# Forgetting heads' queries and keys stored once per pair of heads; latent projections one chunk earlier

## The chip, the cores and the metric

The kernel runs on one core of one Trainium2 chip, as one launch. The metric is the time of that launch on the device in microseconds (us). Engine names are those of the profile: PE is the matrix engine and PEld its weight load, DVE the vector engine, ACT the scalar engine, POOL the general-purpose engine, SP the engine that issues nearly all transfers here (in the trace its issues are called SPq).

## The reference, cut to what matters

Two layers, each a mixer and a mixture of experts, over 1024 tokens of width 1024 in float32. The mixer has 16 heads of width 64: eight forgetting heads, whose scores get a decay from a running sum of log forget gates, and eight latent heads, whose queries, keys and values come from two small latents.

```python
proj = xn @ w_in                      # 3*512 forgetting q, k, v; 8 forget logits; latents of 256 and 128; 32 rope
log_f_cum = jnp.cumsum(log_sigmoid(f_logit + b_f), axis=1)
fox = causal_block_attention(fq, fk, fv, log_f_cum)      # s = q.k * scale + cum[q] - cum[k], softmax, values
q  = rms_norm(c_q) @ w_uq             # 8 heads of 64, plus 32 with rotary
kv = rms_norm(c_kv) @ w_ukv           # 8 heads of 64 keys and 64 values
mla = causal_block_attention(concat(q_nope, rot(q_rope)), concat(k_nope, rot(k_rope)), v)
h = h + concat(rms_norm(fox), rms_norm(mla)) @ w_o
h = h + hierarchical_moe(rms_norm(h), ...)               # 32 experts, two per token
```

## The kernel before, in words

Every float32 matrix product is done as three products of a high and a low part: the helper `split` (L181) makes them, the high part on ACT, the low part as a difference on DVE, and `mm3` (L190) issues the three products (L194, L195, L196). The order on PE, ACT, DVE and POOL is the order in which the program is written; transfers are issued by SP, one after the other.

A mixer goes through these stages, and the change touches the middle ones:

1. Norm, transposes and the small columns of `w_in`, into `xT[0]` and `xT[1]` (high and low parts of the normed input, transposed).
2. Six chunks of 256 columns of `w_in`, in the order v, v, q, q, k, k (L746). Each q or k chunk has four steps of 24 products of 512 columns: two pairs of heads by two halves of the tokens. After a step, `take` (L777) splits its 128 rows (two heads) into a staging tile `st` and writes them to DRAM. While a chunk is computed, `prepare` loads and splits the weights of the next one.
3. Between the steps, work is taken from a queue `jobs`: first the forget gates, latents and value scaling, and from the first k chunk on, when `late_pools` (L664) has opened their space, the latent projections: four loads of `w_uq`, two of `w_ukv`, and 20 projections (`nope` L722, `rope_a` L704, `rope_b` L714), whose results go to DRAM through the same kind of staging tile, called MQ, MQR and MK there.
4. After the last step, the operands of head 0 are loaded (`load_ops`, L806), the latent heads' values are computed in eight blocks of three products (L827 to L832), each copied out by ACT and scanned for its maximum by DVE (`v_take`), and head 1's operands are loaded. Two heads' operands fit at a time (`ops`, two buffers).
5. Attention: per unit of work, scores `S` (L873), row maximum `nm` (DVE, L885), exponential (ACT, L894), transposes (L902), values (L916). Head h+2 is loaded when head h's scores are done.

For forgetting head h the scores are two passes. The first contracts over 128 rows: the queries' high part twice, against the keys' low and high parts. The second contracts over 68 rows: the queries' low part against the keys' high part, and four rows that carry the decay and rows of ones. `FQ` and `FK` in DRAM hold these rows per head as they will be loaded: for the queries 64 rows high, 64 rows high again, 64 rows low, 4 rows; for the keys 64 low, 64 high, 4 rows. So each head's queries are written as two transfers out of 64 rows of `st` (L786, L787), and loaded as one of 128 rows and one of 68 rows (L810 to L813):

```python
                move(o[:, 0], FQ[h, 0:2 * HD])          # 128 rows
                move(o[:, 2], FK[h, 0:2 * HD])
                move(o[0:HD + 4, 1], FQ[h, 2 * HD:])    # 68 rows
                move(o[0:HD + 4, 3], FK[h, HD:])
```

A latent head is loaded as four transfers of 64 or 32 rows with the high and low parts side by side (L816 to L819). The operands' space is that of `xT[1]`, so the load of head 0 waits for the last product that reads it. Eight semaphores are shared by all transfers of SP, so a transfer also waits for the one eight before it.

Of the kernel before, what the change touches and what calls it, by code (L numbers as in the profile page):

```python
# [10 lines left out]
F32R = mybir.dt.float32r  # L11
# [9 lines left out]
P = 128  # L21
T = 1024
# [4 lines left out]
H = 8  # L27
# [54 lines left out]
def kernel(ctx: ExitStack, tc: tile.TileContext, x, positions, attn_norm, w_in, b_f, q_norm, w_uq,  # L82
# [283 lines left out]
    def mixer(l, opened):  # L366
        h_in = [xv[i] for i in range(NT)] if l == 0 else h_d[2 * l - 1]
        h_out = h_d[2 * l]

        FQ = dram.tile([H, 3 * HD + 4, T], F32R, name=f"FQ{l}")  # L370
        FK = dram.tile([H, 2 * HD + 4, T], F32R, name=f"FK{l}")
        MQ = dram.tile([H * HD, 2, T], F32R, name=f"MQ{l}")
        MQR = dram.tile([H * RD, 2, T], F32R, name=f"MQR{l}")
        MK = dram.tile([H * HD, 2, T], F32R, name=f"MK{l}")
# [191 lines left out]
        def forget_d(c):  # L566
            ps = pp.tile([P, 512], F32, name="ps")
            for i in range(4):
                pe.transpose(ps[0:H, i * P:(i + 1) * P], fl["cum"][:, 4 * c + i], ident)
            cs = slice(c * 512, c * 512 + 512)  # L570
            for dst, sgn in ((FQ[:, 3 * HD + 2:, cs], None), (FK[:, 2 * HD:2 * HD + 2, cs], -1.0)):
                st = stg.tile([P, 2, 512], F32R, name="st")[0:H]
                split(st[:, 0], st[:, 1], ps[0:H], sgn)
                move(dst, st)
# [83 lines left out]
            return [v_max, *gap, lambda: v_scale(g, tp)] + [lambda i=i: v_split(g, i, src) for i in range(NT)]  # L658

        one = trix[0:H, None, P:].to_broadcast([H, 16, P])  # L660
        for dst in (FQ[:, 3 * HD:3 * HD + 2], FK[:, 2 * HD + 2:]):
            move(dst.rearrange("h r (c t) -> h (r c) t", t=P), one)

        def late_pools():  # L664
# [74 lines left out]
            for i, (j, c) in enumerate(jc):  # L739
                jobs.append(lambda j=j, c=c: rope_a(j, c))  # L740
                jobs.extend(qj[2 * i:2 * i + 2])
                jobs.append(lambda j=j, c=c: rope_b(j, c))
            jobs.extend(kj)

        late = {}
        chunks = [("v", 0), ("v", 1), ("q", 0), ("q", 1), ("k", 0), ("k", 1)]  # L746
# [3 lines left out]
        for ci, (nm, half) in enumerate(chunks):  # L750
            _, wh, wl = cur
            nxt = prepare(base[chunks[ci + 1][0]] + 256 * chunks[ci + 1][1]) if ci + 1 < len(chunks) else None
            if (nm, half) == ("k", 0):
                late_pools()
            if nm == "v":
                al = slice(0, 256)
                for i in range(NT):
                    ps = pp.tile([P, 512], F32, name="ps")
                    ts = slice(i * P, (i + 1) * P)
                    mm3(ps[:, :256], lambda k: xT[0][:, k, ts], lambda k: xT[1][:, k, ts],  # L760
                        lambda k: wh(k, al), lambda k: wl(k, al), range(KC))
                    if i % 2:
                        run(nxt[0], 2)
                    run(jobs, 2 if i % 2 else 1)
                    v_take(vraw[:, i, half * 256:half * 256 + 256], ps[:, :256], half * NT + i)
                if half == 1:
                    jobs.extendleft(reversed(v_jobs(0, vraw, pp, [lambda: None] * 2)))
            else:
                for s in range(4):
                    j, c = 2 * half + s // 2, s % 2  # L770
                    js, cs = slice((s // 2) * P, (s // 2 + 1) * P), slice(c * 512, c * 512 + 512)
                    ps = pp.tile([P, 512], F32, name="ps")
                    mm3(ps, lambda k: wh(k, js), lambda k: wl(k, js),
                        lambda k: xT[0][:, k, cs], lambda k: xT[1][:, k, cs], range(KC))
                    if nxt:
                        run(nxt[0], 2)
                    def take(nm=nm, j=j, cs=cs, ps=ps):  # L777
                        st = stg.tile([P, 2, 512], F32R, name="st")
                        if nm == "q":
                            split(st[:, 0], st[:, 1], ps, FOX_SCALE)  # L780
                        else:
                            split(st[:, 1], st[:, 0], ps)
                        for e in range(2):
                            h, rs = 2 * j + e, slice(e * HD, (e + 1) * HD)
                            if nm == "q":
                                move(FQ[h, HD:3 * HD].rearrange("(b r) t -> r b t", r=HD)[:, :, cs], st[rs])  # L786
                                move(FQ[h, 0:HD, cs], st[rs, 0])  # L787
                            else:
                                move(FK[h, 0:2 * HD].rearrange("(b r) t -> r b t", r=HD)[:, :, cs], st[rs])

                    if ci == len(chunks) - 1 and s == 3:
                        break
                    take()
                    run(jobs, 4 if nm == "k" else 3)
            cur = nxt
        ring_close()
        xp_close()
# [8 lines left out]
        def load_ops(hh):  # L806
            h = hh % H
            o = ops.tile([P, 4, T], F32R, name="op")
            if hh < H:
                move(o[:, 0], FQ[h, 0:2 * HD])  # L810
                move(o[:, 2], FK[h, 0:2 * HD])
                move(o[0:HD + 4, 1], FQ[h, 2 * HD:])
                move(o[0:HD + 4, 3], FK[h, HD:])  # L813
                return ((o[:, 0], o[:, 2], P), (o[:, 1], o[:, 3], HD + 4))
            hs, rs = slice(h * HD, (h + 1) * HD), slice(h * RD, (h + 1) * RD)
            move(o[0:HD, 0:2], MQ[hs])  # L816
# [2 lines left out]
            move(o[HD:MD, 2:4], MKR)  # L819
            return ((o[:, 0], o[:, 2], MD), (o[:, 0], o[:, 3], MD), (o[:, 1], o[:, 2], MD))  # L820

        opnd = {0: load_ops(0)}
        take()
        uk = late["uk"]
        mx8 = small.tile([P, 2 * NT], F32, name="mx8", bufs=2)
        dve.memset(mx8[:, 0:NT], 0.0)
        for i in range(NT):  # L827
# [2 lines left out]
            mm3(ps, lambda k: ckT[0][:, ts], lambda k: ckT[1][:, ts], lambda k: uk[0][:, 512:1024],  # L830
                lambda k: uk[1][:, 512:1024], [0])
            v_take(vraw2[:, i], ps, NT + i)  # L832
        run(jobs, len(jobs))
        opnd[1] = load_ops(1)
        late["close"]()
        raws_close()
# [859 lines left out]
```

## Time and profile before

| What | us |
|---|---|
| three runs | 1952.24, 1957.9, 1958.68 (median 1957.9) |
| the profiled execution | 1960.09 |
| its span, first to last instruction | 1958.3 |

The profile is of one execution; 1.8 us of it lie outside the span. Its engine line gives busy time, share of the span and number of instructions. In the timeline a row has a start, a duration, the engine, the line, the operation, the tiles (written <- read), partitions x elements, how many instructions were merged, and in brackets how long the engine sat idle before it and for whom. In a table by windows each engine has its busy time (with instructions in brackets), and the last columns are the granted clock of PE as a share of 2.4 GHz, the mean busy share of the 16 DMA engines and the GB/s that they moved.

### The profile page before, as it was taken

To read this page: it belongs to the slowest core of one execution; us is meant where nothing else is said; L and a number is where in the kernel's file an instruction comes from. 1 tells how busy PE (TensorE), PEld (TensorE's weight loads), DVE (VectorE), ACT (ScalarE), POOL (GpSimd) and SP (SyncE) were. 2 spreads that over 40 slices of the span, in tenths; PEclk is the share of its full clock that TensorE was granted. 3 is DMA by queue.
4 is the path that set the end of the run, shared out by engine and by line. 5 is a ranking of instruction groups with operands and counts; after the bars stand their busy time and mean duration, and the time that the engine had idled before them with its cause. 6 is when DMAs were issued, how large, how long until landed. Compare 5 with 4: busy or idle time off the path is not lost.

```text
span 1958.3 us, 33744 instructions
## 1 busy us (share of the span) xinstructions
PE 1745.1 (89%) x12509; PEld 1410.6 (72%) x12509; DVE 1366.3 (70%) x2172; ACT 1185.7 (61%) x2254; POOL 588.1 (30%) x857
## 2 busy tenths in 40 slices
PE   7999889999995999999499997999999869999960
PEld 6987678888884677666399876888878647776540
DVE  6463478888346999888565345888853579988865
ACT  4443378888212889888444335888851258987751
POOL 4001144233204343332231021623341333333215
PEclk9999989999997999999799998999999979999985
DMA  5247833453764999999841775344446569999975
GB/s 160 65 120 217 259 133 110 99 120 87 251 204 146 310 356 357 357 355 354 291 151 52 199 243 200 124 108 109 109 169 233 172 228 363 345 354 350 356 294 213
DMA packets 145380, 427.11 MB, mean 218 GB/s; under 512 B 22166, under 2 KB 37564, under 8 KB 142140
## 3 DMA queue, kind: packets, MB, share of 16 engines
q1 hardware_dynamic: 129788, 387.14, 60.1%
q0 software_dynamic: 14336, 33.58, 5.2%
q10 hardware_dynamic: 1088, 4.19, 0.6%
q8 instruction: 100, 1.64, 0.3%
q14 instruction: 68, 0.56, 0.1%
HBM read 347.24 MB, written 94.37 MB: 226 GB/s over the span
## 4 chain that ended last, share of the span: by engine, by line
PE 28%; DMA 14%; DVE 4%; ACT 3%; issue 2%; POOL 1%; SPq 0%; POOLq 0%; ACTq 0%; DVEq 0%
DMA gu<-in_w_gate_dram 5%; PE ps L194 5%; PE ps L195 5%; PE ps L196 5%; DMA gu<-in_w_up_dram 4%; PE S L873 4%; PE pt L902 3%; DMA dn<-in_w_down_dram 2%; PE y L916 2%; ACT pr L894 1%; DVE nm L885 1%; PE gu L195 1%; PE gu L196 1%; PE gu L194 1%; DMA y<-y 1%
## 5 line engine op out<-in xcount | busy, mean ns | idle before, releaser
L1470 DVE TENSOR_TENSOR lo<-gu,hi 128x1024 fp32r<-128x1024 f32 x248 | 298.6, 1221 | 44.8 <-ACT hi L1469 43.4
L1469 ACT ACTIVATE hi<-gu 128x1024 fp32r<-128x1024 f32 x248 | 258.2, 1059 | 34.5 <-DMA gu<-in_w_up_dram 20.1
L873 PE MATMUL S<-op 96*128 96x512 f32 (+3 forms) x960 | 229.3, 372 | 18.8 <-DMA op<-FK 13.3
L885 DVE TENSOR_REDUCE nm<-S 128x1 f32<-128x1024 f32 (+7 forms) x256 | 183.1, 752 | 68.5 <-PE S L877 68.5
L195 PE MATMUL gu<-lo,V 128*96 128x512 f32 x512 | 205.8, 402 | 11.6 <-DVE lo L1470 11.0
L894 ACT ACTIVATE pr<-S,nm 128x1024 f32<-128x1024 f32 (+7 forms) x256 | 189.2, 755 | 37.3 <-DVE nm L885 37.2
L194 PE MATMUL gu<-hi,V 128*96 128x512 f32 x512 | 206.7, 404 | 1.2 <-ACT hi L1469 0.7
L196 PE MATMUL gu<-hi,V 128*96 128x512 f32 x512 | 203.5, 398 | 1.2 <-DVE V L185 0.6
L904 ACT ACTIVATE ph<-pt 128x512 f16<-128x512 f32 x288 | 157.3, 601 | 66.5 <-PE pt L902 65.6
L905 DVE SCALAR_TENSOR_TENSOR pl<-pt,ph 128x512 f16<-128x512 f32 x288 | 184.7, 682 | 8.7 <-ACT ph L904 7.8
L1519 POOL DMA_INDIRECT y<-V,sidx x64 | 72.1, 1127 | 385.9 <-ACT V L1518 369.4
L873 PEld LDWEIGHTS S<-op 96*128 96x128 f32 (+1 forms) x960 | 161.5, 196 | 36.5 <-DMA wor<-in_w_o_dram 13.6
L1470 DVE TENSOR_TENSOR lo<-dn,hi 128x1024 fp32r<-128x1024 f32 x128 | 156.1, 1221 | 17.0 <-ACT hi L1469 16.4
L902 PE MATMUL pt<-ident,pr 128*128 128x128 f32 x1152 | 155.1, 278 | 8.6 <-ACT pr L894 6.3
L1469 ACT ACTIVATE hi<-dn 128x1024 fp32r<-128x1024 f32 x128 | 135.0, 1056 | 19.8 <-DMA dn<-in_w_down_dram 19.5
L902 PEld LDWEIGHTS pt<-ident,pr 128*128 128x128 f32 x1152 | 125.2, 143 | 13.9 <-ACT pr L894 13.2
L195 PEld LDWEIGHTS gu<-lo,V 128*96 128x96 f32 x512 | 83.2, 162 | 60.4 <-DVE lo L1470 31.0
L916 PE MATMUL y<-V,ph 128*128 128x64 f16 x2304 | 121.6, 193 | 2.8 <-ACT ph L904 1.6
L916 PEld LDWEIGHTS <-ph 128*128 128x128 f16 x2304 | 116.9, 98 | 5.3 <-ACT ph L904 1.8
L916 PE MATMUL y<-V,pl 128*128 128x64 f16 x1152 | 117.0, 193 | 1.1 <-DVE pl L905 1.0
L196 PEld LDWEIGHTS gu<-hi,V 128*96 128x96 f32 x512 | 83.2, 163 | 38.6 <-DVE V L185 7.3
L175 POOL TENSOR_SCALAR rs_v<-ss 128x1 f32<-128x1 f32 (+1 forms) x44 | 21.0, 477 | 287.4 <-ACT xn L1096 149.5
(363 smaller groups left out, 4382.0 us busy)
## 6 DMA issues: line engine op xcount, KB each, us to landing
gu<-in_w_gate_dram SPq DMA_DIRECT2D x124, 512.0 KB
gu<-in_w_up_dram SPq DMA_DIRECT2D x124, 512.0 KB
dn<-in_w_down_dram SPq DMA_DIRECT2D x60, 1024.0 KB
raw<-in_w_in_dram SPq DMA_DIRECT2D x48, 256.0 KB
h<-ht SPq DMA_DIRECT2D x17, 512.0 KB
FQ<-st SPq DMA_DIRECT2D x32, 256.0 KB
FK<-st SPq DMA_DIRECT2D x32, 256.0 KB
MQ<-st SPq DMA_DIRECT2D x16, 512.0 KB
```

Of the source, the lines that this page charges most:

```text
L194: pe.matmul(ps, sh(kc), mh(kc), start=first and i == 0, stop=False)
L195: pe.matmul(ps, sh(kc), ml(kc), start=False, stop=False)
L196: pe.matmul(ps, sl(kc), mh(kc), start=False, stop=last and i == n - 1)
L873: pe.matmul(o, a[0:k, qs], b[0:k, c0:c0 + n], start=bank not in started, stop=pi == len(passes) - 1 and not diag, skip_group_check=True)
L885: dve.tensor_reduce(nm, u["S"][:, col:col + (qb + 1) * P], axis=AX.X, op=OP.max, negate=True)
L894: act.activation(u["pr"][:, s], u["S"][:, s], AF.Exp, bias=nm, accum_out=zst[h // 2][:, qb, h % 2:h % 2 + 1])
L902: pe.transpose(pt[:, b], u["pr"][:, (4 * q + b) * P:(4 * q + b + 1) * P], ident)
L904: act.activation(u["ph"][:, ks], pt, AF.Copy, scale=P_SCALE)
L905: dve.scalar_tensor_tensor(u["pl"][:, ks], pt, P_SCALE, u["ph"][:, ks], op0=OP.mult, op1=OP.subtract)
L916: pe.matmul(yst[h][:, qb], a[:, b], v[:, kb, h % H, c], start=first_y[h], stop=(kb == qb and s == 2), skip_group_check=True)
L1469: act.activation(h_, raw, AF.Copy)
L1470: eng.tensor_tensor(l_, raw, h_.bitcast(F32), op=OP.subtract)
```

## The change

- `FQ` and `FK` become `[H * 64, 2, T]`, with the high and low parts side by side, as MQ and MK are; the four decay and ones rows go to two small tensors, `FQC` and `FKC`. A `take` is one write of 128 rows, two heads at a time, where it was four writes (queries) or two (keys).
- `load_ops` builds the same tile in SBUF out of six transfers of 64 rows or 4 rows, where there were four of 128 and 68 rows. The rows of the high part that stand twice are now read twice.
- `late_pools` is called ahead of the second q chunk, and three jobs are taken per step in every chunk (it was four per step in the k chunks).
- Four of the eight key projections (blocks 4 to 7) leave the queue: each is done behind one of the first four value blocks.

```diff
-        FQ = dram.tile([H, 3 * HD + 4, T], F32R, name=f"FQ{l}")
-        FK = dram.tile([H, 2 * HD + 4, T], F32R, name=f"FK{l}")
+        FQ = dram.tile([H * HD, 2, T], F32R, name=f"FQ{l}")
+        FK = dram.tile([H * HD, 2, T], F32R, name=f"FK{l}")
+        FQC = dram.tile([H, 4, T], F32R, name=f"FQC{l}")
+        FKC = dram.tile([H, 4, T], F32R, name=f"FKC{l}")
...
-            for dst, sgn in ((FQ[:, 3 * HD + 2:, cs], None), (FK[:, 2 * HD:2 * HD + 2, cs], -1.0)):
+            for dst, sgn in ((FQC[:, 2:, cs], None), (FKC[:, 0:2, cs], -1.0)):
...
-            jobs.extend(kj)
+            jobs.extend(kj[:4])
+            late["kj"] = kj[4:]
...
-            if (nm, half) == ("k", 0):
+            if (nm, half) == ("q", 1):
                 late_pools()
...
-                        for e in range(2):
-                            h, rs = 2 * j + e, slice(e * HD, (e + 1) * HD)
-                            if nm == "q":
-                                move(FQ[h, HD:3 * HD].rearrange("(b r) t -> r b t", r=HD)[:, :, cs], st[rs])
-                                move(FQ[h, 0:HD, cs], st[rs, 0])
-                            else:
-                                move(FK[h, 0:2 * HD].rearrange("(b r) t -> r b t", r=HD)[:, :, cs], st[rs])
+                        move((FQ if nm == "q" else FK)[j * P:(j + 1) * P, :, cs], st)
...
-                    run(jobs, 4 if nm == "k" else 3)
+                    run(jobs, 3)
...
-                move(o[:, 0], FQ[h, 0:2 * HD])
-                move(o[:, 2], FK[h, 0:2 * HD])
-                move(o[0:HD + 4, 1], FQ[h, 2 * HD:])
-                move(o[0:HD + 4, 3], FK[h, HD:])
+                hs = slice(h * HD, (h + 1) * HD)
+                move(o[0:HD, 0:2], FQ[hs])
+                move(o[HD:, 0], FQ[hs, 0])
+                move(o[0:HD, 2:4], FK[hs])
+                move(o[HD:, 2], FK[hs, 1])
+                move(o[HD:HD + 4, 1], FQC[h])
+                move(o[HD:HD + 4, 3], FKC[h])
...
         opnd = {0: load_ops(0)}
         take()
+        run(jobs, len(jobs))
...
             v_take(vraw2[:, i], ps, NT + i)
-        run(jobs, len(jobs))
+            if i < len(late["kj"]):
+                late["kj"][i]()
```

What this does to the order is seen at three places, all in layer 0; layer 1 has the same. On SP, from the end of the q chunks on, before (FQ and FK are the queries and keys in DRAM, `raw` the landing tile of weights, `w_uq` and `w_ukv` the latent weights):

```order
L93 DMA FQ_155<-st 64x2x512
L93 DMA FQ_155<-st 64x512
L686 DMA raw<-in_w_uq_dram 128x256 x2
L733 DMA sinT<-sin_d 128x1024
L505 DMA raw<-in_w_in_dram 128x2x256 x2
L686 DMA raw<-in_w_uq_dram 128x512
L93 DMA FK_156<-st 64x2x512 x2
L686 DMA raw<-in_w_uq_dram 128x512
L686 DMA raw<-in_w_ukv_dram 128x512 x2
```

The same queue now, from the fourth step of the first q chunk to the first step of the second (the first two `w_uq` loads stand further up, among the earlier steps):

```order
L93 DMA FQ_155<-st 256x1x512
L734 DMA cosT<-cos_d 128x1024
L93 DMA MKR_162<-st 64x1x512 x2
L735 DMA sinT<-sin_d 128x1024
L93 DMA FQ_155<-st 256x1x512
L688 DMA raw<-in_w_uq_dram 128x512 x2
L688 DMA raw<-in_w_ukv_dram 128x512
L507 DMA raw<-in_w_in_dram 128x2x256
```

The four latent loads stood behind all writes of the queries; now they stand behind one write of each step. On SP, at the end of the k chunks, before (`op` is the tile of a head's operands, MK the latent keys in DRAM):

```order
L93 DMA FK_156<-st 64x2x512 x2
L93 DMA MK_159<-st 256x1x512 x4
L93 DMA op<-FQ_155 128x1024
L93 DMA op<-FK_156 128x1024
L93 DMA op<-FQ_155 68x1024
L93 DMA op<-FK_156 68x1024
L93 DMA FK_156<-st 64x2x512 x2
L93 DMA op<-FQ_155 128x1024
```

And now:

```order
L93 DMA FK_156<-st 256x1x512 x3
L93 DMA op<-FQ_155 64x2048
L93 DMA op<-FQ_155 64x1024
L93 DMA op<-FK_156 64x2048
L93 DMA op<-FK_156 64x1024
L93 DMA op<-FQC_157 4x1024
L93 DMA op<-FKC_158 4x1024
L93 DMA FK_156<-st 256x1x512
L93 DMA MK_161<-st 256x1x512 x4
L93 DMA op<-FQ_155 64x2048
```

The load of head 0 had four key writes ahead of it and one operand load behind it; now there are the six transfers of head 0, then the last `take` and four key writes, then head 1. On ACT, from the last projections to the first exponential, before (`vraw` is the copy of a value block, `st` a staging tile):

```order
L187 ACTIVATE st<-ps 128x512 x2
L184 ACTIVATE st<-qr 128x512
L184 ACTIVATE st<-ps 128x512 x11
L627 ACTIVATE vraw<-ps 128x512 x8
L894 ACTIVATE pr,zs<-S,nm 128x1024
```

And now, with buffer numbers (`st_2362` is the last `take`; `st_2420` is the fourth of the moved key blocks, and takes over `st_2362`'s buffer):

```order
L184 ACTIVATE st_2362<-ps_2317 128x512
L629 ACTIVATE vraw_2351<-ps_2368 128x512
L184 ACTIVATE st_2378<-ps_2374 128x512
L629 ACTIVATE vraw_2351<-ps_2382 128x512
L184 ACTIVATE st_2392<-ps_2388 128x512
L629 ACTIVATE vraw_2351<-ps_2396 128x512
L184 ACTIVATE st_2406<-ps_2402 128x512
L629 ACTIVATE vraw_2351<-ps_2410 128x512
L184 ACTIVATE st_2420<-ps_2416 128x512
L629 ACTIVATE vraw_2351<-ps_2424 128x512
L629 ACTIVATE vraw_2351<-ps_2430 128x512
L629 ACTIVATE vraw_2351<-ps_2436 128x512
```

The key blocks stood ahead of the value blocks; now four of them stand between the first five, and DVE follows the same order.

## Rows read from the trace of the kernel before

**Rows 1.** The page's engine line: busy us, share, instructions.

```profile
PE 1745.1 (89%) x12509; PEld 1410.6 (72%) x12509; DVE 1366.3 (70%) x2172; ACT 1185.7 (61%) x2254; POOL 588.1 (30%) x857
```

**Rows 2.** Waits of PE, layer 0, 100 to 262: total, times, longest.

```profile
PE S L873 <- DMA op<-FK: 9.9, 2, 7.1
PE ps L194 <- ACT uq L184: 2.7, 2, 1.9
```

**Rows 3.** Waits of PE, layer 1, 1060 to 1212.

```profile
PE S L873 <- DMA wor<-in_w_o_dram: 5.5, 1, 5.5
PE S L873 <- DMA op<-FK: 3.3, 1, 3.3
PE ps L194 <- ACT uq L184: 1.2, 1, 1.2
```

**Rows 4.** Timeline of SP, layer 0: issues of transfers.

```profile
152.27 12.15 SPq L93 DMA_DIRECT2D FQ<-st  x12
...
262.67 0.33 SPq L93 DMA_DIRECT2D op<-FQ  x1
...
332.53 0.34 SPq L93 DMA_DIRECT2D op<-FQ  x1
...
346.79 0.50 SPq L93 DMA_DIRECT2D op<-MQ  x1
```

**Rows 5.** Table by windows: writes, latent weights, attention's start (250:255).

```profile
125.00:130.00 5.00, 5.00 (x24) 4.09 (x23) 2.16 (x7) 2.00 (x4) 0.00 (x0) 1.00 0.78 196
175.00:180.00 5.00, 3.37 (x9) 2.43 (x10) 1.38 (x2) 1.26 (x2) 0.00 (x0) 0.79 0.46 138
180.00:185.00 5.00, 5.00 (x21) 4.01 (x20) 3.72 (x7) 3.10 (x6) 1.44 (x2) 0.87 0.52 137
220.00:225.00 5.00, 5.00 (x23) 4.10 (x23) 1.00 (x2) 1.53 (x3) 0.00 (x0) 1.00 1.02 376
250.00:255.00 5.00, 4.74 (x20) 3.96 (x18) 3.05 (x5) 2.67 (x5) 0.00 (x0) 0.50 0.34 129
1125.00:1130.00 5.00, 3.77 (x16) 2.44 (x15) 1.31 (x2) 1.24 (x2) 0.00 (x0) 1.00 0.53 179
```

**Rows 6.** Timeline of PE, layer 0: value blocks and first scores.

```profile
231.49 0.40 PE L194 MATMUL ps<-uk,ck 128*128 128x512 f32 x1
...
236.75 0.39 PE L196 MATMUL ps<-uk,ck 128*128 128x512 f32 x1
239.97 0.77 PE L873 MATMUL S<-op 128*128 128x512 f32 x1 [2.83 <-DMA op<-FK]
247.82 1.62 PE L873 MATMUL S<-op 68*128 68x512 f32 x3 [7.09 <-DMA op<-FK]
```

**Rows 7.** Timeline of DVE, layer 0: a key split, seven maxima, the first row maximum.

```profile
230.98 0.69 DVE L185 TENSOR_TENSOR st<-ps,st 128x512 fp32r<-128x512 f32 x1 [2.44 <-ACT st L184]
...
234.78 4.27 DVE L628 TENSOR_REDUCE mx<-ps 128x1 f32<-128x512 f32 x7
249.61 1.23 DVE L885 TENSOR_REDUCE nm<-S 128x1 f32<-128x1024 f32 x1 [10.56 <-PE S L877]
```

**Rows 8.** The same two ends in layer 1: PE's last value block.

```profile
1187.90 0.39 PE L196 MATMUL ps<-uk,ck 128*128 128x512 f32 x1
```

**Rows 9.** And DVE's first row maximum in layer 1.

```profile
1199.70 1.23 DVE L885 TENSOR_REDUCE nm<-S 128x1 f32<-128x1024 f32 x1 [9.52 <-PE S L877]
```

**Rows 10.** Table by windows: loads of a forgetting head, then of a latent head.

```profile
265.00:267.00 2.00, 2.00 (x20) 1.48 (x20) 1.82 (x3) 1.76 (x5) 1.90 (x3) 1.00 0.96 375
267.00:273.00 6.00, 6.00 (x95) 5.55 (x92) 5.09 (x9) 5.19 (x13) 0.33 (x2) 1.00 0.26 94
...
348.00:355.00 7.00, 6.47 (x85) 5.57 (x84) 5.76 (x10) 6.01 (x14) 0.48 (x2) 1.00 1.00 221
```

**Rows 11.** Timeline of ACT, layer 0: a key's high part, eight copies of values.

```profile
230.35 0.60 ACT L184 ACTIVATE st<-ps 128x512 fp32r<-128x512 f32 x1 [2.65 <-DMA FK<-st]
...
233.42 4.35 ACT L627 ACTIVATE vraw<-ps 128x512 f32<-128x512 f32 x8
```

More of the change, by code (lines that the diff above doesn't have):

```diff
@@ L660, in mixer @@
         one = trix[0:H, None, P:].to_broadcast([H, 16, P])
-        for dst in (FQ[:, 3 * HD:3 * HD + 2], FK[:, 2 * HD + 2:]):
+        for dst in (FQC[:, 0:2], FKC[:, 2:]):
             move(dst.rearrange("h r (c t) -> h (r c) t", t=P), one)
```

## The prediction

> **What bounds the kernel now.** I read the engine line first, then the waits of PE in the two stretches that the change touches, then their timelines. PE is busy for 89% of the span, more than any other engine [rows 1], so time is won where PE stands still or runs at the lower clock, and moving work between engines wins nothing. From the first chunk of columns to the first unit of attention PE waits at two places only. The latent weights hold it for 2.7 us in layer 0 and 1.2 us in layer 1; the operands of head 0 hold it for 9.9 us (2.83 and 7.09) and 8.8 us (3.3 and 5.5; the row that names `wor` can't be right, since scores read `op` alone, so it is the second half of the load) [rows 2, 3]. The reader is to see two causes. First, SP spends 12.15 us on twelve query writes at 152 to 164 [rows 4]; the first latent loads stand right behind them in its queue. Second, the load of head 0 stands behind four key writes, and its last two parts have 68 rows.
>
> What a transfer costs is read by its number of rows. While forgetting queries are written out of 64 rows of a staging tile, the DMA engines are 78% busy and move 196 GB/s, 251 per full share; while keys go out, mostly in 128-row writes, it is 1.02 and 376 GB/s. Of a forgetting head's load, the 128-row parts move at 375 GB/s; behind them the 68-row parts take six more microseconds at a share of 0.26 and 94 GB/s, as four of sixteen engines would. A latent head's load, all of 64 and 32 rows, keeps the share at 1.00 and moves 221 GB/s for 7 us, 1.55 MB [rows 5, 10].
>
> The Trainium skill (DMA: Bandwidth & Descriptors, "Why a DMA increments its semaphore by 16 and not by 1") says that a transfer is spread over the largest number of engines up to 16 that divides the outermost sizes: 4 for 68 rows, 16 for 64. The trace agrees with its 0.26.
>
> **Latent weights.** Now there is one write of 0.5 MB per step in place of four of 0.75 MB together, at 376 GB/s 1.3 us of a step that lasts 24 products of 0.229 us (5.26 us in 23 intervals between the first and last value product [rows 6]), or 5.5 us. That removes nothing from PE, it only empties the queue. The first two `w_uq` loads are issued a chunk before they are needed; the other two follow the write of step one of the second q chunk, and their first use comes after another step and a projection, 5.5 + 1.4 us later. In between are the take's split (0.60 on ACT, 0.69 on DVE [rows 7, 11]), the write, the two loads and their own splits: about 1.5 + 1.3 + 2 + 2 us. I cost it at 0.2 us per layer, between 0 and 1; ACT then stands behind the `w_ukv` loads, but PE has eight PSUM tiles to fill meanwhile. What goes: 2.7 + 1.2 us, and the clock after the stall of layer 0: granted 0.79 and 0.87 in 175 to 185, (0.21 + 0.13) x 5 = 1.7 us. Layer 1's stall of 1.2 us shows 1.00 [rows 5] and costs no clock. Sum 5.6 - 0.4 = 5.2 us.
>
> **Start of attention.** I measure from the end of PE's last value product to the start of the first row maximum `nm`, from which the pipeline is the same before and after. Before: 236.98 to 249.61, 12.6 us, and 1188.13 to 1199.70, 11.6 us [rows 6 to 9] (0.23 is added to the last product's start). PE's total work ahead is the same now, since the four key blocks are only moved.
>
> After, let 0 be the end of the last step, where the load of head 0 may start (it stands behind three key writes that are done). PE has 36 products of 0.229, so its value blocks end at 8.2. The load is 1.5 MB in parts of 64 rows and two of 4 rows. Its nearest row is the latent head: issued at 346.79, done at 355, 8.3 us [rows 4, 10]; bounds are the 128-row rate, 1.2 us until data plus 1.5 MB at 375 GB/s = 5.2, and the present forgetting head, 262.67 to 273, 10.3. I take 8.4.
>
> That is hidden, but what stands behind it isn't. The last `take`'s write is issued behind the six parts. Its data move after theirs (0.5 MB at 376 GB/s, 1.4 us) and its completion is seen later; no row shows how much, between 0 and 1.5; I take 0.8: 10.6. The fourth moved key block takes over that staging buffer, so ACT waits at it until 10.6, in order, and with it the copies of value blocks 4 to 7; DVE's split and four maxima stand behind. So 10.6, ACT 0.60, DVE 0.69, four maxima of 0.61 (4.27 / 7), and 0.1 for hand-overs: `nm` at 14.4, 6.2 us after PE's last value block. A stall of this kind is seen already: ACT's wait of 2.65 for a key write at 230 [rows 7, 11]. The scores themselves wait for maxima too, so they start no earlier than about 12 or 13; PE stands still for some 4 us where it was 9.9. Gain 12.6 - 6.2 = 6.4 and 11.6 - 6.2 = 5.4, sum 11.8 us.
>
> The clock is 0.50, its lower level of 1.2 GHz, in 250 to 255 before, worth up to 2.5 us per layer if no dip were left [rows 5]; PE will still wait some 4 us, more than the 2.7 that cost clock in layer 0. I take 0.5 per layer, between 0 and 2.5.
>
> The Trainium skill speaks against this part (SBUF — State Buffer, "Door 1: The DMA port swizzle"): 64 partitions reach half of the ports, and two transfers to disjoint halves serialize. The 221 against 375 GB/s agrees. If rows of 64 moved at the full rate, the load would end 3 us earlier, and the sum would be about 6 us more.
>
> **Loads inside attention.** Twelve later loads of forgetting heads (heads 2 to 7 of both layers) change from 10.3 to about 8.4 us plus two more issues of 0.4. Five heads take 332.53 - 262.67 = 69.9 us, 14 each [rows 4]; both are covered, and this is worth nothing. Head 1's load is issued only behind the blocked key write, at about 12.5, behind three key writes of 1.4, and lands near 24; it is needed for the fifth unit, about 11 to 12 us after `nm`, at 25 to 26. It is covered by 1 to 2 us; I cost it at nothing, and at 2 us per layer if the pipeline starts faster.
>
> **Sum.** 5.2 + 11.8 + 1.0 = 18.0. The profiled execution took 1960.1, 2.2 above the median of 1957.9. So 1942.1, or 1939.9 against the median: 1940 us.
>
> **Rivals.**
>
> A. The buffer doesn't bind: the last write completes early because its packets don't queue behind the load. For it: writes read SBUF and loads write it; against: both use the same 16 engines, at a share of 1.00. Then DVE's thirteen operations (five splits of 0.69, eight maxima of 0.61, from 0.8) end at 9.1, scores and `nm` follow at 10.0, 4.4 us earlier in each layer: 1940 - 8.8 = 1931.
>
> B. The buffer binds harder: load of 10.3, completion 1.5 late, latent weights 1 us late, head 1 late by 1 us, no clock gained: 2 x (1.9 + 0.7 + 0.8 + 1 + 0.5) = 9.8, so 1950.
>
> C. The time is given back: the experts are bound by their weights' transfers. Against it: these start when attention's buffers come free, so they move with it. Then 1958, no change.
>
> D. Slower: inside attention the six parts of a head's load are late in every head. The place is the wait of scores for `op`; it decides from 14 us on, the time of a head. Latent rows (8.3) and present ones (10.3) speak against it. At 17 us, as if the parts ran one after the other twice over, twelve heads wait 3 us each: 36 - 18 = 18 slower, 1976.
>
> **How the numbers follow.** Forecast (1936 to 1946) 0.56, A 0.18, B 0.15, C 0.06, D 0.05. A measurement here can tell about 0.3%, 6 us. B's far end touches that bound, so faster is 0.56 + 0.18 + 0.14 = 0.88, same 0.07, slower 0.05. The range takes in A and B with the clock's bound: 1927 (A with 2 us of clock per layer) to 1951; left out are C and D and their neighbours.
>
> **What would show it.** PE's waits for `uq` under 1 us in both layers, with no dip of the clock near 180. In the value blocks, ACT's wait on a staging tile for FK, then a key split and four maxima on DVE, and `nm` some 6 us behind PE's last value block. Head loads at full share near 220 GB/s without a tail at 0.26. Wrong would be: `nm` at 2 us (A), over 8 us (B), waits of scores for `op` from head 1 on (D), or both stages shorter while the whole is not (C).

## The result, and the profile after

The changed kernel takes 1942.5 us (median; 1941.7 to 1944.8) where the kernel before, beside it, takes 1956.9: a ratio of 0.993, with a 95% interval of 0.9914 to 0.9946. The profiled execution took 1944.8 us, 15.3 less than that of before. It is faster by 0.7%, and 2.5 us above the forecast of 1940.

The engine line of the page, to set against [rows 1]: PE's share rises a point, since it stands still for less time at the same work.

```profile
PE 1739.6 (90%) x12509; PEld 1408.7 (73%) x12509; DVE 1370.2 (71%) x2172; ACT 1184.5 (61%) x2254; POOL 607.1 (31%) x857
```

PE's waits from the first chunk to the first units of attention, as in [rows 2, 3]; layer 0 first, layer 1 behind the dots (total us, times, longest):

```profile
PE S L876 <- DVE mx L630: 4.8, 1, 4.8
PE ps L194 <- ACT uq L184: 1.2, 1, 1.2
...
PE S L876 <- DVE mx L630: 4.1, 1, 4.1
PE S L876 <- DMA op<-FK: 1.3, 1, 1.3
PE S L876 <- DMA op<-FKC: 0.5, 1, 0.5
PE ps L194 <- ACT uq L184: 0.2, 1, 0.2
```

The latent weights hold PE for 1.4 us in all, where it was 3.9. At attention's start PE now waits chiefly for the maxima of DVE; the load still holds it in layer 1, for 1.8 us. Why DVE is late, ACT's timeline says (layer 0, to be set against [rows 11]; the last row is the same block in layer 1):

```profile
225.81 0.60 ACT L184 ACTIVATE st<-ps 128x512 fp32r<-128x512 f32 x1 [4.84 <-PE ps L196]
...
230.61 0.60 ACT L629 ACTIVATE vraw<-ps 128x512 f32<-128x512 f32 x1
236.78 0.60 ACT L184 ACTIVATE st<-ps 128x512 fp32r<-128x512 f32 x1 [5.56 <-DMA FK<-st]
...
1185.07 0.60 ACT L184 ACTIVATE st<-ps 128x512 fp32r<-128x512 f32 x1 [6.35 <-DMA FK<-st]
```

The first row is the split behind the last step; the step itself ends 0.2 us earlier, at 225.61. The row at 236.78 is the fourth moved key block; ACT stands 5.56 us at it for a key write, and the copies of the value blocks stand behind. That write was issued behind the load, here in layer 1 (the issues of the first two parts and of the write):

```profile
1173.08 1.14 SPq L93 DMA_DIRECT2D op<-FQ  x2
...
1176.81 0.57 SPq L93 DMA_DIRECT2D FK<-st  x1
```

DVE, against [rows 7, 9]; the last two rows are of layer 1:

```profile
237.41 0.69 DVE L185 TENSOR_TENSOR st<-ps,st 128x512 fp32r<-128x512 f32 x1 [5.47 <-ACT st L184]
238.01 2.47 DVE L630 TENSOR_REDUCE mx<-ps 128x1 f32<-128x512 f32 x4
240.99 1.22 DVE L888 TENSOR_REDUCE nm<-S 128x1 f32<-128x1024 f32 x1 [0.51 <-PE S L880]
...
1185.70 0.69 DVE L185 TENSOR_TENSOR st<-ps,st 128x512 fp32r<-128x512 f32 x1 [6.25 <-ACT st L184]
1188.70 1.22 DVE L888 TENSOR_REDUCE nm<-S 128x1 f32<-128x1024 f32 x1
```

And PE, against [rows 6, 8]: its first and last value product, then the first scores, in layer 0 and in layer 1.

```profile
225.61 0.40 PE L194 MATMUL ps<-uk,ck 128*128 128x512 f32 x1
...
233.59 0.39 PE L196 MATMUL ps<-uk,ck 128*128 128x512 f32 x1
238.75 2.07 PE L876 MATMUL S<-op 128*128 128x512 f32 x4 [4.77 <-DVE mx L630]
...
1173.12 0.40 PE L194 MATMUL ps<-uk,ck 128*128 128x512 f32 x1
...
1181.10 0.39 PE L196 MATMUL ps<-uk,ck 128*128 128x512 f32 x1
1182.79 0.47 PE L876 MATMUL S<-op 128*128 128x512 f32 x1 [1.30 <-DMA op<-FK]
1183.73 0.93 PE L876 MATMUL S<-op 68*128 68x512 f32 x3 [0.47 <-DMA op<-FKC]
1188.84 1.86 PE L876 MATMUL S<-op 128*128 128x512 f32 x4 [4.11 <-DVE mx L630]
```

With 0.23 for the last product, `nm` starts 240.99 - 233.82 = 7.2 us behind it in layer 0 and 1188.70 - 1181.33 = 7.4 in layer 1; before it was 12.6 and 11.6. Windows, against [rows 5, 10] (the last columns are granted clock, DMA share and GB/s):

```profile
150.00:155.00 5.00, 3.83 (x16) 2.44 (x15) 1.35 (x2) 1.26 (x2) 0.00 (x0) 1.00 0.39 119
175.00:180.00 5.00, 5.00 (x24) 4.09 (x23) 2.20 (x5) 1.79 (x3) 0.66 (x1) 1.00 0.89 284
...
235.00:240.00 5.00, 1.25 (x3) 1.06 (x4) 2.60 (x5) 2.56 (x5) 0.00 (x0) 0.70 1.02 393
240.00:245.00 5.00, 4.74 (x18) 3.53 (x18) 3.00 (x4) 1.55 (x3) 0.00 (x0) 0.50 1.04 264
245.00:250.00 5.00, 3.90 (x34) 3.27 (x33) 3.95 (x8) 4.24 (x11) 0.00 (x0) 0.78 0.96 221
...
284.00:287.00 3.00, 3.00 (x43) 2.69 (x41) 2.47 (x4) 2.01 (x5) 2.90 (x3) 1.00 1.09 244
```

The stall for the latent weights no longer takes the clock down (1.00 at 150 to 155 and at 175 to 180). The start of attention still does: 0.70, 0.50, 0.78. A later head's load (issued at 280) keeps a full share at 244 GB/s and shows no tail at 0.26.

Where the time went can be read from equal PE instructions in both traces. The first step of layer 0 is 0.4 us later than before; its last value product is 3.2 us earlier, `nm` 8.6, the last values of attention 8.9. In layer 1 the first chunk is 5.9 us earlier, the last value product 6.8, `nm` 11.0, the end of attention 11.3, the end of the span 15.3. So the stages that the change touches gave 3.6 + 5.4 + 0.3 in layer 0 and 1.0 + 4.2 + 0.3 in layer 1, 14.8 us. Elsewhere some time was lost (1.7 in layer 0's experts, 1.3 in the norm ahead of layer 1's chunks) and a little more gained (2.2 in layer 1's experts, 1.8 in the end of the kernel); the change touches none of these, and no run here looks for their causes.

### The profile page after: what moved, and what is told of

Its sections match the earlier page's. It is cut to its first block, busy times and chain, and to the rows that moved or that the text cites. A ratio compares the mean times of both kernels' runs of the same rounds, so it can differ in the third digit from the quotient of the medians.

```text
span 1943.0 us, 33657 instructions
## 1 busy us (share of the span) xinstructions
PE 1739.6 (90%) x12509; PEld 1408.7 (73%) x12509; DVE 1370.2 (71%) x2172; ACT 1184.5 (61%) x2254; POOL 607.1 (31%) x857
## 4 chain that ended last, share of the span: by engine, by line
PE 33%; DMA 9%; DVE 4%; ACT 3%; POOL 1%; issue 1%; SPq 0%; POOLq 0%; ACTq 0%; DVEq 0%
PE ps L194 5%; PE ps L195 5%; PE ps L196 5%; PE S L876 4%; DMA dn<-in_w_down_dram 3%; PE pt L905 3%; PE gu L195 2%; PE gu L196 2%; PE gu L194 2%; DMA gu<-in_w_up_dram 2%; DMA gu<-in_w_gate_dram 2%; PE y L919 2%; PE py L195 1%; PE py L194 1%; PE py L196 1%
## 5 line engine op out<-in xcount | busy, mean ns | idle before, releaser
L876 PE MATMUL S<-op 96*128 96x512 f32 (+3 forms) x960 | 227.3, 370 | 10.7 <-DVE mx L630 8.9
L195 PE MATMUL gu<-lo,V 128*96 128x512 f32 x512 | 205.0, 400 | 11.2 <-DVE lo L1473 11.2
L1522 POOL DMA_INDIRECT y<-V,sidx x64 | 83.6, 1306 | 371.0 <-ACT V L1521 353.9
```

Source lines behind the costliest of these rows:

```text
L195: pe.matmul(ps, sh(kc), ml(kc), start=False, stop=False)
L876: pe.matmul(o, a[0:k, qs], b[0:k, c0:c0 + n], start=bank not in started, stop=pi == len(passes) - 1 and not diag, skip_group_check=True)
```

## The experiments

The theory was the prediction's: the last step's write goes out behind head 0's load, a key block needs its staging tile, and so ACT, DVE and the scores wait. Its rivals: the load alone binds, or the storage does all of it. For each kernel the table has two distances: from the end of the last step (ACT's first split behind it; before: the first value product, which in the other kernels stands 0.2 us ahead of that split) to `nm`, in layer 0 and layer 1, and how many of PE's products lie in that stretch and are hidden in it (0.229 us each). A product outside of it has to be paid elsewhere, so the two are read together.

| kernel | us | ratio (95%) | last step to `nm` | products | last value product to `nm` |
|---|---|---|---|---|---|
| before | 1956.9 | | 18.1, 17.1 | 24 | 12.6, 11.6 |
| changed | 1942.5 | 0.993 (0.9914 to 0.9946) | 15.2, 15.4 | 36 | 7.2, 7.4 |
| e4 storage only | 1943.8 | 0.9934 (0.991 to 0.9958) | 12.1, 12.3 | 24 | 6.9, 7.0 |
| e5 order only | 1954.1 | 0.9989 (0.9977 to 1.0002) | 16.2, 15.8 | 36 | 8.2, 7.8 |
| e1 all keys queued | 1945.7 | 0.9939 (0.992 to 0.9958) | 12.0, 11.8 | 24 | 6.7, 6.5 |
| e2 write first | 1940.0 | 0.9906 (0.9877 to 0.9936) | 12.8, 12.3 | 36 | 4.8, 4.3 |
| a2 changed, again | 1945.7 | 0.9932 (0.9915 to 0.9949) | 15.7, 15.4 | 36 | 7.7, 7.4 |
| e8 own buffer | 1938.0 | 0.9898 (0.9881 to 0.9916) | 11.6, 11.1 | 33 | 4.2, 3.7 |
| e7 storage, write first | 1945.4 | 0.9924 (0.9906 to 0.9942) | 13.6, 13.4 | 24 | 8.3, 8.1 |
| e6 rows in two halves | 2134.0 | 1.09 (1.088 to 1.092) | | | |
| e9 alternating rows | 1935.9 | 0.9877 (0.9854 to 0.9899) | 9.6, 10.7 | 33 | 2.2, 3.4 |
| e10 projections late | 1934.9 | 0.9872 (0.9851 to 0.9893) | 11.1, 10.9 | 33 | 3.8, 3.5 |
| e11 all together | 1930.4 | 0.9855 (0.9837 to 0.9874) | 10.2, 10.1 | 33 | 2.8, 2.8 |

Times are medians, each beside runs of the kernel before; kernels are compared by their ratios.

**Storage alone and order alone.** e4 has the new tensors, writes and loads, and the projections and key blocks where they were before (its edit to the changed kernel is below); e5 is the reverse, the storage of before with the new order.

```diff
-            jobs.extend(kj[:4])
-            late["kj"] = kj[4:]
+            jobs.extend(kj)
+            late["kj"] = []
...
-            if (nm, half) == ("q", 1):
+            if (nm, half) == ("k", 0):
                 late_pools()
...
-                    run(jobs, 3)
+                    run(jobs, 4 if nm == "k" else 3)
```

> The storage part alone: queries and keys stored once, two heads to a transfer, six parts per load; the jobs in the order of before (late_pools at the first k chunk, four per step, all key blocks queued). Theory (the stall on latent weights came from SP and the DMA engines being full of query writes, and the load's tail from the 68-row parts): the waits for uq shrink to under 1 us in layer 0 even without the earlier call, the first row maximum stands about 9 us behind PE's last value product (four key writes and then 9.7 us of load, against 5.5 us of value blocks); about 8 to 10 us faster than before, near 1948. Rival (the order is what helps): less than 4 us faster than before.

> The order part alone: latent projections from the second q chunk on, four key blocks among the values; queries and keys stored and loaded as before. Theory: the DMA engines are fuller in the second q chunk (0.75 MB of queries per step at half rate beside latent writes), so PE waits for latent weights again, 1 to 4 us per layer; the load of head 0 ends with its 68-row parts near 10 to 11 us, the last key write behind it, and the fourth moved block waits for it as in the changed kernel: first row maximum 7 to 9 us behind the last value product; 4 to 9 us faster than before, near 1951. Rival (storage is what helps): within 2 us of before.

The storage alone gives all of the gain that can be measured (0.9934 beside 0.993), more than was expected of it; the order alone is no change within what these runs can tell. PE's waits say why. The latent weights' wait is gone in e4 (PE waits for nothing between 100 and 230), and grows to 4.6 us in e5, whose writes are as many as before (3.3 in layer 1):

```profile
155.51 0.80 PE L194 MATMUL ps<-cq,uq 128*128 128x512 f32 x1 [4.63 <-ACT uq L184]
```

At attention's start, however, the order alone is not worth nothing. From PE's last value product to `nm`, e5 gains 4.4 + 3.8 = 8.2 us on the kernel before, e4 5.8 + 4.6 = 10.3, and both together 9.6: each half does most of this alone, so the two gains don't add up. What e5 gains there it gives back in part at the latent weights, whose waits are 4.0 us longer than before.

**Which wait sets the start.** e1 queues all key blocks, so that none meets the last write's tile; its edit is the first four lines above. e2 writes the last `take` ahead of head 0's load in the program; on SP the write then stands behind the first of the load's six parts and ahead of the other five:

```diff
-        opnd = {0: load_ops(0)}
         take()
+        opnd = {0: load_ops(0)}
```

> All eight latent key blocks stay in the queue of jobs (done between the k steps); none among the values; all else as in the changed kernel. Theory (the staging buffer of the last key write, which stands behind head 0's load, holds ACT, and with it the maxima): no wait of ACT for FK among the value blocks; the first row maximum some 4 to 5 us after PE's last value product, set by the load of head 0 (about 10 us from its issue), where it is 7.2 and 7.4 now; about 2.5 us faster per layer, 5 in all, near 1938. Rival (the load of head 0 alone sets the start, the buffer only hides behind it): the first row maximum stays at 7 us or more, and the time stays near 1943.

> The changed kernel with the last take (split and key write) written ahead of the load of head 0, so that the write stands ahead of the load on SP. Theory: the fourth moved key block no longer waits (under 1 us on ACT for FK); the load is issued about 1.7 us later and ends at 11 to 12 after the last step; first row maximum about 4.5 us behind PE's last value product, 5 us in all faster, near 1938. Rival (the load alone sets it): the load's later issue shows in full, the time is 3 us longer, near 1946.

In e1 ACT's wait is gone, and the scores wait for the load instead. The rows are PE's first scores and DVE's `nm`, layer 0:

```profile
237.95 2.38 PE L876 MATMUL S<-op 128*128 128x512 f32 x4 [3.97 <-DMA op<-FK]
...
240.50 1.23 DVE L888 TENSOR_REDUCE nm<-S 128x1 f32<-128x1024 f32 x1 [5.16 <-PE S L880]
```

From the last step to `nm` it is 3.2 and 3.6 us shorter than in the changed kernel, as the theory wants; but twelve products, 2.75 us, no longer lie under the load. What is left is 0.5 and 0.9 us per layer, and the time stays. The theory's wait was real, and its time of 1938 was wrong, since it left out that the key blocks are the load's cover. e2 keeps that cover and shortens the wait (ACT still stands 1.1 and 1.2 us for FK): 2.4 and 3.1 us less per layer, 1940.0 where 1938 was expected. Its interval overlaps that of the changed kernel, so the time alone doesn't show a gain.

**The buffer by itself.** e8 leaves SP's order at this place as it is (the load, the last write, the key writes) and only sees to it that no key block takes over the last write's tile. The staging tiles of the projections come from two groups in turn, and the added job passes one turn. One key block fewer stands among the values:

```diff
-            jobs.extend(kj[:4])
-            late["kj"] = kj[4:]
+            jobs.extend(kj[:5])
+            jobs.append(lambda: turn.__setitem__(0, turn[0] + 1))
+            late["kj"] = kj[5:]
```

> The changed kernel itself, on the chip that times the next three, so that they can be compared with it. Expected: about 1942.5 us, ratio to before 0.993 as in its first runs; in the profile the first row maximum again 7 to 7.5 us behind PE's last value product in both layers, with ACT waiting 5 to 6.5 us for the write of a key staging tile.

> Three key blocks instead of four stand among the value blocks, and none of them uses the staging buffer of the last step's write; the order of head 0's parts, the last write and the key writes on SP is that of the changed kernel. Theory (the buffer binds: the last write waits behind head 0's load, and a key block waits for the write): ACT's wait of 5.6 and 6.4 us for FK<-st goes, scores then wait for the load alone, which lands 10 to 11 us after the last step ends, nm stands 4 to 5 us behind PE's last value product instead of 7.2 and 7.4, and the time is 1942.5 - 2 x 2.7 = 1937 us. Rival (the load alone binds, the buffer was hidden beside it): nm does not move against the end of the last step, 7.5 us or more behind the last value product, and the time stays at 1942 to 1943 us.

a2 repeats the changed kernel's wait, 6.1 and 6.3 us on ACT. e8 is what the theory said: ACT's wait for FK is gone, `nm` stands 3.4 and 3.6 us nearer to the last value product than in a2, and the time is 7.7 us below a2's on the same chip (5.4 were expected; that 1938.0 lies so near to the 1937 of the expectation is in part luck, since that sum began at 1942.5). Its interval meets that of a2, 0.9915 to 0.9949, only at the ends. The first scores and `nm` in layer 0, then the first scores in layer 1:

```profile
235.12 0.47 PE L877 MATMUL S<-op 128*128 128x512 f32 x1 [1.94 <-DVE mx L630]
235.82 1.28 PE L877 MATMUL S<-op 68*128 68x512 f32 x3 [0.23 <-DMA op<-FKC]
...
237.26 1.22 DVE L889 TENSOR_REDUCE nm<-S 128x1 f32<-128x1024 f32 x1 [2.73 <-PE S L881]
...
1175.65 1.46 PE L877 MATMUL S<-op 128*128 128x512 f32 x4 [2.01 <-DMA op<-FK]
```

What is late next is the load: issued at 225.45, its last part is there at 235.8.

**Do two loads share?** After e1 I held that head 1's load, issued straight behind head 0's, slows it. e7 (e4 with e2's edit) was to show it.

> The storage of the changed kernel with the projections where the kernel before had them, all key blocks in the queue, and the last step's write issued ahead of head 0's load. Theory (with no key writes between them the loads of heads 0 and 1 share the engines, and that sets the start): the order of the last write changes nothing, scores wait 4 to 5 us for op<-FK, nm stays 6.5 to 7.5 us behind the last value product as with the storage alone (6.9 and 7.0), 1943 to 1945 us. Rival (the last write is what costs, whatever stands behind it): nm 4 to 5 us behind the last value product, as where the write was put first in the changed kernel (4.8 and 4.3), and 1939 to 1940 us.

The time is that of e4, as the theory said, but its reason falls. The trace records when each transfer's last completion was counted. From the first issue to that of the last part, head 0's load takes 10.3 and 10.1 us in e1 and 10.5 and 10.4 in e4, with head 1's load behind it; 10.2 and 10.1 in e8, with four writes behind it; and the twelve later loads of forgetting heads in the changed kernel, with no head's load behind them for 12 us, take 9.8 to 10.5. What is issued behind a load costs it nothing that shows. In e7 scores start at 237.59, 11.6 us after the first issue at 226.01, because the write now stands inside the load:

```profile
226.01 0.51 SPq L93 DMA_DIRECT2D op<-FQ  x1
227.59 0.52 SPq L93 DMA_DIRECT2D FK<-st  x1
...
237.59 2.05 PE L876 MATMUL S<-op 128*128 128x512 f32 x4 [5.89 <-DMA op<-FK]
```

So the write inside the load costs 1.5 and 1.1 us (13.6 and 13.4 against 12.1 and 12.3), which is worth it only where a key block waits for that write, as in e2.

**What a row costs.** e6 and e9 load the same bytes with two transfers of 128 rows and two of 64 in place of four of 64. e6 (on e2) takes the 128 rows as two halves:

```diff
-                move(o[0:HD, 0:2], FQ[hs])
-                move(o[HD:, 0], FQ[hs, 0])
-                move(o[0:HD, 2:4], FK[hs])
-                move(o[HD:, 2], FK[hs, 1])
+                move(o[:, 0], FQ[hs, 0][None].to_broadcast([2, HD, T]))
+                move(o[:, 2], FK[hs].rearrange("r b t -> b r t"))
+                move(o[0:HD, 1], FQ[hs, 1])
+                move(o[0:HD, 3], FK[hs, 1])
```

e9 (on e8) takes them as alternating rows, with 64 and 128 as the outermost sizes; its first two new lines are these, the other two are those of e6:

```diff
+                move(o[:, 0], FQ[hs, 0][:, None].to_broadcast([HD, 2, T]))
+                move(o[:, 2], FK[hs].rearrange("r b t -> (r b) t"))
```

> The last step's write first, and head 0's operands loaded as two transfers of 128 rows (the queries' high part read twice, the keys' low and high part from the same storage), two of 64 and two of 4 rows, the same bytes. Theory (a transfer's rate goes by its rows, 375 GB/s with 128 against 221 with 64): 1.0 MB at 375 and 0.5 MB at 221 take 2.8 + 2.3 = 5.1 us where all parts of 64 rows take 7.0, so the load lands 1.9 us earlier; in layer 1, where scores waited 2.8 us for it, nm comes 1 to 2 us earlier, in layer 0, where they waited for maxima, 0.2; 1937 to 1939 us against 1940.0. Rival (the rate goes by the bytes alone, or by the 64 rows of the source in memory): within 1 us of 1940. A second rival (the outermost size of 2 spreads a transfer over 2 of 16 engines, 47 GB/s): 1 MB takes 21 us, every forgetting head waits some 10 us, over 2000 us.

> As e8_own_buffer, but head 0's and every later forgetting head's operands lie in the tile with high and low rows alternating, so that the keys' two parts come as one transfer of 128 rows from 128 consecutive rows, and the queries' high part as one transfer to 128 rows (64 source rows, each read twice); two transfers of 64 rows and two of 4 rows remain, the same bytes. Theory (the rate goes by the rows of SBUF that a transfer spans, where its outermost size can be spread over all engines): the parts of 128 rows move at 375 GB/s, the load of head 0 lands 1.9 us earlier, in layer 1 scores stop waiting for it (2.0 us in e8), in layer 0 they wait for maxima as before; 1936 us against 1938.0, and a loaded window shows over 300 GB/s. Rival (the rate is that of the source's rows or of the bytes): 241 GB/s as before and 1938 us.

e6 met its second rival. A window of one of its later loads, then PE's wait over the whole span:

```profile
283.00:290.00 7.00, 7.00 (x75) 6.02 (x75) 4.93 (x7) 4.29 (x9) 0.48 (x2) 0.76 0.14 54
...
PE S L876 <- DMA op<-FK: 138.7, 16, 16.5
```

A share of 0.14 and 54 GB/s is what two of sixteen engines would do. The Trainium skill (DMA: Bandwidth & Descriptors, "Why a DMA increments its semaphore by 16 and not by 1") says that a transfer is spread over the largest number of engines up to 16 that divides the outermost sizes of both of its sides; with an outermost size of 2 that is two, and the trace agrees. With 64 or 128 outermost, in e9, the load is faster. While the first parts move, e8 (64 rows), then e9 (128 rows) in the same window, then e9 when its 64-row parts follow (the end of a 128-row part is still in it):

```profile
229.00:231.00 2.00, 2.00 (x11) 1.65 (x10) 2.00 (x4) 1.76 (x4) 0.00 (x0) 1.00 1.14 244
```

```profile
229.00:231.00 2.00, 2.00 (x11) 1.65 (x10) 2.00 (x4) 1.76 (x4) 0.00 (x0) 1.00 0.97 371
231.00:233.00 2.00, 2.00 (x11) 1.65 (x10) 2.00 (x4) 1.76 (x4) 0.00 (x0) 1.00 1.01 209
```

And the last part of the load, as PE sees it: e9 in layer 0 and in layer 1, then e8's weight load in layer 1.

```profile
234.58 0.94 PE L877 MATMUL S<-op 68*128 68x512 f32 x3 [0.80 <-DMA op<-FK]
...
1177.41 0.94 PE L877 MATMUL S<-op 68*128 68x512 f32 x3 [1.40 <-DMA op<-FK]
```

```profile
1176.15 0.53 PEld L877 LDWEIGHTS S<-op 68*128 68x128 f32 x3 [0.35 <-DMA op<-FQC]
```

The 128-row parts move at 371 GB/s, the 64-row parts at 244 and 209, at a full share. In layer 0 the last part lands 234.58 - 225.81 = 8.8 us after the first issue where e8 takes 10.4: 1.6 of the 1.9 expected. In layer 1 it is only 1177.41 - 1167.52 = 9.9 against 1176.15 - 1165.91 = 10.2. Over the twelve later loads of forgetting heads the median, by the record of completions, goes from 10.3 to 9.5 us, so 0.9 us describes it better than 1.6. The expectation had the layers the wrong way round: `nm` gained 2.0 us in layer 0 and 0.4 in layer 1. As a time, 1935.9 cannot be told from e8's 1938.0.

**The projections' place, and everything together.** e10 is e8 with `late_pools` at the first k chunk and four jobs per step; e11 is e9 with the same.

> As e8_own_buffer, but the latent projections begin with the first k chunk and run four to a step, as in the kernel before; the storage of the changed kernel stays. Theory (the wait for the latent weights went because half of the bytes written and fewer writes stand ahead of their loads, so the storage alone takes it away): PE waits under 0.5 us for uq in both layers, as with the storage alone (0 and 0), the time is that of e8 within 2 us, 1937 to 1940. Rival (the earlier start of the projections carries that part): waits of 2.7 and 1.2 us and a clock below 1.00 behind the one of layer 0, 5 us longer than e8, 1943.

> The last two runs together: the alternating rows of e9_interleaved_rows and the projections where the kernel before had them, as in e10_projections_late. Theory (the load's rate and the latent weights' wait are separate terms, and both hold): no wait of PE for uq, nm 2.3 to 3.4 us behind the last value product, 1933 to 1935 us, ratio to before 0.985 to 0.988. Rival (the projections placed late put more key writes ahead of head 0's load, which takes back what its rate gives): nm 4 us or more behind, 1936 to 1938 us.

e10 has no wait for `uq` in either layer and is no slower than e8 (0.9872 and 0.9898). So the storage removed that wait, and the earlier start of the projections carries nothing; it brought 1.2 and 0.2 us back, which e4 and e10 don't have. e11 has the lowest time: 1930.4 us, 0.9855 (0.9837 to 0.9874), below the changed kernel by more than both intervals, though e9 and e10 alone can't be told from it. Its scores follow PE's last value product (231.53) at once, and only the second half waits, for the last part of the load:

```profile
231.77 0.40 PE L877 MATMUL S<-op 128*128 128x512 f32 x1
...
233.54 0.93 PE L877 MATMUL S<-op 68*128 68x512 f32 x3 [1.37 <-DMA op<-FKC]
```

## Why the prediction was right, and where its terms were off

**The sum.** The prediction had 18.0 us of gain for the profiled execution; 15.3 were measured, 14.8 of them in the stages that it spoke of. The direction and the places were right, and each step has its row. All three terms came out smaller than forecast, so nothing cancelled; 0.5 us net came from stages that the change does not touch.

**Latent weights: 5.2 forecast, 4.6 measured** (3.6 and 1.0). No dip of the clock is left near 180, and the waits went from 3.9 to 1.4 us. In layer 0 1.2 us remain where 0.2 was put, just over the bound of 1 (0.6 in a2). The reason was half right: the queue was emptied by the new writes (e4), and not by moving the loads forward, which alone makes the wait longer (e5).

**Start of attention: 11.8 forecast, 9.6 measured** (5.4 and 4.2, from `nm` at 7.2 and 7.4 behind PE's last value product instead of 6.2). The mechanism is the one that was forecast: ACT waits for the write behind the load, then come the split, four maxima, the scores. Its second half was sized well: from ACT's start to `nm` 4.2 and 3.6 us, 3.8 forecast. In layer 1 the first scores did not wait for the maxima but for the load, at 1182.79; `nm` stood behind the maxima all the same. The first half is the mis-sized term. ACT was to go on 10.6 us after the step's end; it went on at 236.78 - 225.61 = 11.2 in layer 0 and at 1185.07 - 1173.12 = 12.0 in layer 1. The load was put at 8.4 us, by the nearest row, that of a latent head, which was read as done at 355 [rows 10]. Data still moved after that in the kernel before:

```profile
355.00:356.00 1.00, 0.91 (x18) 0.80 (x16) 0.82 (x3) 0.93 (x3) 0.00 (x0) 1.00 0.20 41
```

and the record of completions has the last part of that load at 356.7, 9.9 us after its issue, not 8.3 (and 355 - 346.79 is 8.2). The readers of a load went on at its last completion: for head 0 in layer 1 of the changed kernel the record has it at 1183.6, and the scores go on at 1183.73. So it took 10.7 us, from 1173.08 on, and the upper bound of 10.3 was the better value. That is 2.3 us too little in layer 1, and 0.9 of it came back: ACT goes on 1.3 us behind the load's last part, where 2.2 was assumed (1.4 for the write's data, and 0.8 for a completion that no row had shown).

**Rival A** (the buffer doesn't bind) is out: ACT's waits of 5.6 and 6.4 us are in the trace, and e8, which takes the buffer away, gains. It would not have reached A's 10.0 us after the step either: e8 has `nm` 11.8 and 11.3 us behind the step's end, since the load is then the limit. **Rival B** (it binds harder) had the right sign for this term: `nm` 7.2 to 7.4, between 6.2 and the 8 at which B was to be believed.

**The clock: 1.0 forecast, at most 0.6 measured** (0.3 per layer from `nm` to the end of attention, beyond what is in the other terms; no run separates the clock in it). The dip is still there: the granted clock is 0.70, 0.50 and 0.78 around a pause of PE of 4.8 us.

**Loads inside attention: nothing forecast, nothing seen.** No row of PE's waits in layer 0's attention names `op`; the longest single wait there is 1.1 us. So rival D fell. C fell too: what was lost in layer 0's experts is 1.7 us of 8.9 gained, and the whole is 15.3 shorter.

**What the rule on 64 rows was worth.** The Trainium skill (SBUF — State Buffer, "Door 1: The DMA port swizzle") was cited against this part; e9 shows that the price is real, 244 against 371 GB/s while the first parts move, but smaller than the 3 us put on it: with two thirds of the bytes in 128 rows, 1.6 and 0.3 us of head 0's load and 0.9 of a later one.

## What to carry to other kernels

Writing data once, in the largest transfers the tile allows, paid here through what stood in the queue behind the writes; whether by their number or their bytes was not told apart. Read a load as done at its last completion: for the latent head's load that was 1.7 us behind the end of the window of full share. When work is moved in front of a load to cover it, look at which buffers that work takes over: a buffer whose last write stands behind the same load turns the cover into a wait. Compare such versions by the distance from a fixed event and by the work hidden in it, since either alone misleads (e1).

## What the runs showed of the hardware

- A transfer whose outermost size is 2 ran at a share of 0.14 and 54 GB/s, although it fills 128 rows of the tile; the same rows in alternating order, 64 and 128 outermost, moved at 371 GB/s (e6; e9, 229 to 231).
- What was issued straight behind a load did not make that load later: by the record of completions 10.1 to 10.5 us with a second load behind it (e1, e4), 10.1 and 10.2 with four writes behind (e8), 9.8 to 10.5 with no head's load behind for 12 us (the changed kernel's later loads).
- A write of 0.5 MB issued behind 1.5 MB of loads was seen as done only behind them: ACT, which waited for it, went on 11.2 and 12.0 us after the end of the step that made its data, in layer 1 1.3 us behind the load's last part.
